# Seven block products for eight in the gated linear unit and the down projection, with the first pair of each FFN made plain

## The chip, the cores and the metric

The kernel runs on one core of one Trainium2 chip. Its metric is the device time of one execution in microseconds (us). The engines are named as the profile names them: PE multiplies matrices (PEld is its weight load), DVE and ACT work on vectors, POOL is GpSimd, and SP issues most of the loads.

## The reference

Two blocks run one after the other on `x` of 256 rows and 2048 columns, in fp32. The first has a state-space mixer whose output goes through a gated linear unit (GLU), an attention over dilated windows, and after each of them a feed-forward network (FFN). The second has two layers of a mixer of its own kind, which the change doesn't touch. What it touches, cut down:

```python
def swiglu_ffn(h, w_gate_up, w_down):            # d = 2048, d_ff = 5632
    gate, up = jnp.split(h @ w_gate_up, 2, axis=-1)
    return (jax.nn.silu(gate) * up) @ w_down

def s5_mixer(u, a_re, a_im, log_dt, b_re, b_im, c_re, c_im, d_skip, w_glu):
    ...
    g = jax.nn.gelu(y).astype(u.dtype)           # y: the outputs of the scan
    val, gate = jnp.split(g @ w_glu, 2, axis=-1)
    return (val.astype(f32) * jax.nn.sigmoid(gate.astype(f32))).astype(u.dtype)

def first_block(x, ...):
    for layer in range(2):
        h = rmsnorm(x, mix_norm[layer])
        x = x + (s5_mixer(h, ...) if layer == 0 else dilated_attention(h, ...))
        x = x + swiglu_ffn(rmsnorm(x, ffn_norm[layer]), w_gate_up[layer], w_down[layer])
    return x
```

## The kernel before, in words

**Stages.** The program is one stream: the state-space mixer (`s5`, lines 405 to 890), the GLU (893 to 911), the FFN of layer 0 (328 to 356), the attention, the FFN of layer 1, and the two mixers of the second block. `x` stays in the core's memory as 2 row halves of 128 rows. For a product, 128x128 blocks of it are transposed on PE, and gain and split make the left operand: a k-tile is 128 of the 2048 columns.

**Products.** Every fp32 operand is split in two parts, hi (a cast on ACT) and lo (a subtraction on DVE), so that a product takes three matmuls: hi times hi, hi times lo of the weights, lo times hi. `gemm` (55 to 90) makes one block of 512 columns: 16 k-tiles, 2 row halves, 3 matmuls, 96 in all (lines 69, 70, 71), into 2 of the 4 banks of the pool `psg`. Its weights come in `load_unit` (30 to 47) as 4 k-tiles a load of 1 MB, by SP into 2 buffers `wraw`, and are split 2 k-tiles at a time (42, 43) into 4 buffers each of `whi` and `wlo`.

**Seven for eight.** `Strassen.gemm_pair` (144 to 221) makes two blocks of 512 columns together. Of 4 k-tiles, 12 to 15, it takes 2x2 blocks (row halves, and even and odd k-tiles, on the left; even and odd k-tiles, and the two column blocks, on the right) and forms seven products of sums of blocks where eight plain ones would stand, each 6 matmuls (168 to 170). The sums of weights are DVE subtractions into `wt` (3 buffers), split like weights (140, 141). Four intermediate results are copied out of their bank by ACT (line 174) into `st_p1`, `st_p7`, `st_u2` and `st_u4`, one buffer each, because the bank goes on to sum. The other 12 k-tiles are plain (212 to 214, 144 matmuls): 186 matmuls for a pair, where two calls of `gemm` have 192. At the end DVE adds the four copies to the four banks.

**The FFN.** Before its first product `x_transposed` (306 to 324) transposes k-tiles 12 to 15 first (line 315), makes of them the left operands of the seven products (`x_pair`, 112 to 133, with the copies and sums on ACT and DVE), and then transposes k-tiles 0 to 11 (line 259). There are 11 chunks of 512 columns of d_ff, in groups of 4, 4 and 3. Each chunk is a `gemm_pair` of a gate block and an up block; its product, `m`, is transposed during the next pair (8 transposes, `meanwhile`). After a group the down projection runs four plain calls of `gemm` over the 16 (last group 12) k-tiles of the group, and each adds its two banks to `x` (line 355). The GLU runs 8 plain calls.

**Order.** A scheduler that works by priority lays out each engine's instructions, and each engine runs its own in order. `meanwhile` and `start` queue work, of which a call of a product takes pieces as it goes; `behind` puts an instruction after another one. The weight loads of a next product are issued when a buffer is free.

**State-space mixer.** It starts with loads on two queues: four of `x` on SP (447, 448), six small ones (`dt`, `ai`, `ar`) on ACT's queue, and then on ACT's queue the gains and `b_re`, `b_im`. At its end DVE runs a serial scan, while PE makes kernel matrices, which go through memory (`kp`) into `M` (795, 798); then PE makes the outputs from `M` (`own`) and from the scan's states (`states`), and ACT and DVE split them for the GLU. `load_x` (800) loads `x` anew behind that.

## Time and profile before

| | |
|---|---|
| median of 3 runs | 3247.86 us (3246.82 to 3248.42) |
| the profiled execution, its own time | 3248.64 us |
| its span in the profile | 3246.5 us |
| granted TensorE clock, mean | 0.994 |
| busy: PE, DVE, ACT | 97%, 65%, 51% of the span |
| HBM read | 568.51 MB, 176 GB/s |

The span is the time from the first to the last instruction, 2.1 us less than the execution. Busy shares count overlapping work of several engines, each by itself. A pipelined matmul's listed duration reaches beyond the start of the next one, so the pace of matmuls is taken from the distance of starts. In a timeline row, brackets give how long the engine had been idle and what released it. The clock column is 1.00 where PE was granted its full 2.4 GHz throughout.

### The profile page before, as it was taken

What the parts mean: (1) busy time and instruction counts of PE and PEld (TensorE: products, weight loads), DVE (VectorE), ACT (ScalarE), POOL (GpSimd) and SP (SyncE); (2) the same over time, 40 slices, a digit from 0 to 9 for tenths busy, and PEclk for the clock granted to TensorE, in tenths of its full rate; (3) what the DMA queues carried; (4) which work ended last, traced back from release to release, by engine and by line L of the source; (5) the groups of instructions that cost most, each with busy time, mean ns of one, the idle gap of its engine ahead of it and who ended that gap; (6) DMA issues with size and microseconds to landing.
All of it is one profiled execution on the core that took longest, in us unless ns stands there. A gap on an engine that the chain in (4) does not pass through costs nothing.

```text
span 3246.5 us, 43041 instructions
## 1 busy us (share of the span) xinstructions
PE 3162.5 (97%) x16950; PEld 2689.0 (83%) x16961; DVE 2121.9 (65%) x3244; ACT 1668.9 (51%) x2247; POOL 13.7 (0%) x23
## 2 busy tenths in 40 slices
PE   4999999999999999999989999999999999999998
PEld 4788788888888888888878888888889888899887
DVE  8955776576575666756778757756657566575565
ACT  6344654455454555545555545545456455564463
POOL 1000000000000000000000000000000000000000
PEclk9999999999999999999999999999999999999999
DMA  3265456555555555454555646555555546556554
GB/s 72 59 214 191 141 207 208 195 194 195 190 176 199 169 171 176 159 189 162 169 163 195 205 169 207 205 188 203 172 175 166 190 151 214 162 165 194 161 185 168
DMA packets 341675, 573.93 MB, mean 177 GB/s; under 512 B 53537, under 2 KB 105249, under 8 KB 340641
## 3 DMA queue, kind: packets, MB, share of 16 engines
q1 hardware_dynamic: 306944, 561.84, 52.7%
q10 hardware_dynamic: 34528, 9.35, 1.4%
q8 instruction: 133, 2.18, 0.3%
q14 instruction: 70, 0.57, 0.1%
HBM read 568.51 MB, written 2.62 MB: 176 GB/s over the span
## 4 chain that ended last, share of the span: by engine, by line
PE 92%; ACT 3%; DVE 2%; DMA 2%; issue 1%; ACTq 0%; another core or an unknown queue 0%; DVEq 0%; SPq 0%
PE psg L71 19%; PE psg L69 19%; PE psg L70 19%; PE psg L214 7%; PE psg L213 7%; PE psg L212 7%; PE psg L168 2%; PE psg L169 2%; PE psg L170 2%; PE psm L378 2%; PE psg L378 1%; PE psm L259 1%; PE psm L1012 1%; DMA wraw<-in_w_in 1%; ACT act_hi L268 1%
## 5 line engine op out<-in xcount | busy, mean ns | idle before, releaser
L43 DVE TENSOR_TENSOR wlo<-wraw,whi 128x1024 fp32r<-128x1024 f32 (+1 forms) x752 | 863.5, 1155 | 727.6 <-ACT whi L42 723.2
L42 ACT CAST whi<-wraw 128x1024 fp32r<-128x1024 f32 (+1 forms) x752 | 744.3, 997 | 941.4 <-PE psg L71 664.0
L69 PE MATMUL psg<-whi,act_hi 128*128 128x512 f32 (+1 forms) x2912 | 1101.4, 378 | 0.8 <-DVE act_lo L378 0.7
L71 PE MATMUL psg<-whi,act_lo 128*128 128x512 f32 (+1 forms) x2912 | 1094.4, 376 | 0.2
L70 PE MATMUL psg<-wlo,act_hi 128*128 128x512 f32 (+1 forms) x2912 | 1093.8, 376 | 0.0
L71 PEld LDWEIGHTS psg<-whi,act_lo 128*128 128x128 f32 x2912 | 546.8, 188 | 85.9 <-issue 1.3
L69 PEld LDWEIGHTS psg<-whi,act_hi 128*128 128x128 f32 x2912 | 547.2, 188 | 85.4 <-issue 1.3
L70 PEld LDWEIGHTS psg<-wlo,act_hi 128*128 128x128 f32 x2912 | 547.3, 188 | 81.9
L141 DVE TENSOR_TENSOR wlo<-wraw,whi 128x1024 fp32r<-128x1024 f32 x330 | 393.6, 1222 | 225.8 <-ACT whi L140 224.9
L140 ACT CAST whi<-wraw 128x1024 fp32r<-128x1024 f32 x330 | 339.6, 1054 | 328.5 <-DMA wraw<-in_w_gate_up 171.3
L212 PE MATMUL psg<-whi,act_hi 128*128 128x512 f32 x1056 | 412.2, 390 | 0.0
L214 PE MATMUL psg<-whi,act_lo 128*128 128x512 f32 x1056 | 411.1, 389 | 0.0
L213 PE MATMUL psg<-wlo,act_hi 128*128 128x512 f32 x1056 | 410.9, 389 | 0.0
L214 PEld LDWEIGHTS psg<-whi,act_lo 128*128 128x128 f32 x1056 | 198.2, 188 | 41.2
L212 PEld LDWEIGHTS psg<-whi,act_hi 128*128 128x128 f32 x1056 | 198.3, 188 | 40.8
L213 PEld LDWEIGHTS psg<-wlo,act_hi 128*128 128x128 f32 x1056 | 198.3, 188 | 40.8
L141 DVE TENSOR_TENSOR wlo<-wt,whi 128x1024 fp32r<-128x1024 f32 x88 | 107.3, 1220 | 33.3 <-ACT whi L140 33.3
L168 PE MATMUL psg<-whi,xf_hi 128*128 128x512 f32 x308 | 122.1, 405 | 6.8 <-ACT st_p L174 5.8
L140 ACT CAST whi<-wt 128x1024 fp32r<-128x1024 f32 x88 | 92.8, 1054 | 66.0 <-PE psg L214 36.5
L169 PE MATMUL psg<-wlo,xf_hi 128*128 128x512 f32 x308 | 123.5, 401 | 0.0
L170 PE MATMUL psg<-whi,xf_lo 128*128 128x512 f32 x308 | 122.4, 398 | 0.2 <-DVE xf_lo L131 0.2
L168 PEld LDWEIGHTS psg<-whi,xf_hi 128*128 128x128 f32 x308 | 59.2, 192 | 23.0 <-ACT st_p L174 6.6
(350 smaller groups left out, 2374.4 us busy)
## 6 DMA issues: line engine op xcount, KB each, us to landing
wraw<-in_w_gate_up SPq DMA_DIRECT2D x352, 512.0 KB, 4.7
wraw<-in_w_down SPq DMA_DIRECT2D x88, 1024.0 KB, 5.0
wraw<-in_w_in SPq DMA_DIRECT2D x96, 768.0 KB, 4.6
wraw<-in_w_q SPq DMA_DIRECT2D x48, 1024.0 KB, 5.2
wraw<-in_w_glu SPq DMA_DIRECT2D x32, 1024.0 KB, 5.4
wraw<-in_w_kv SPq DMA_DIRECT2D x32, 1024.0 KB, 5.4
wraw<-in_w_in SPq DMA_DIRECT2D x32, 1024.0 KB, 5.1
wraw<-in_w_out SPq DMA_DIRECT2D x32, 1024.0 KB, 5.1
```

The costliest lines, as they stand in the source:

```text
L42: k.act_at = nc.scalar.copy(hi[:, :n, :cw], raw[:, a:a + n, :cw]).ins
L43: k.dve_at = nc.vector.tensor_tensor(lo[:, :n, :cw], raw[:, a:a + n, :cw], hi[:, :n, :cw].bitcast(F32), ALU.subtract).ins
L69: nc.tensor.matmul(o, a, wh, start=n == 0, stop=False)
L70: nc.tensor.matmul(o, a, wl, start=False, stop=False)
L71: k.mm = nc.tensor.matmul(o, b, wh, start=False, stop=n == total - 1).ins
L140: k.act_at = nc.scalar.copy(hi, src).ins
L141: k.dve_at = nc.vector.tensor_tensor(lo, src, hi.bitcast(F32), ALU.subtract).ins
L168: nc.tensor.matmul(o, a, wh[:, q], start=start and q == 0, stop=False, skip_group_check=True)
L169: nc.tensor.matmul(o, a, wl[:, q], start=False, stop=False, skip_group_check=True)
L212: nc.tensor.matmul(o, a, wh[:, n], start=False, stop=False, skip_group_check=True)
L213: nc.tensor.matmul(o, a, wl[:, n], start=False, stop=False, skip_group_check=True)
L214: k.mm = nc.tensor.matmul(o, b, wh[:, n], start=False, stop=end, skip_group_check=True).ins
```

## The change

It does five things.

1. The GLU's last three column blocks go through `gemm_pair` (gate and value block as the pair); the first stays plain.
2. The down projection goes through `gemm_pair` twice a group, on column blocks 0 and 1, then 2 and 3. Its block k-tiles are the first four of the group, whose sums (`mf`) are made as soon as the group's first chunk is transposed. With `apart`, the four kept copies aren't added to the banks: copies and banks are each added to `x`, 8 DVE additions a pair in place of 4.
3. The first pair of each FFN is plain (`gemm` for gate, `gemm` for up). The sums for the later ones are made beside it by the new `forms`, from the finished hi and lo. Single blocks (A11, A12, A22) are taken from the operand itself.
4. `load_x` goes behind the first GLU product, and the first GLU weights are issued behind the last load of `M` (`k.sp_at`).
5. The six small loads at the start go from ACT's queue to SP's, ahead of `x`.

The pieces of queued work in `gemm_pair` are now taken once after the seven products and after every fourth direct k-tile.

```diff
 in gemm:
-        with behind(k, k.lo_at):
+        with behind(k, k.lo_at), behind(k, k.sp_at):
             parts = load_unit(k, W, g[0][1], len(g), c0, cw)
 in Strassen (x_forms and x_pair are removed):
+    def forms(self, xT, kt0, name):
+        k, nc = self.k, self.k.nc
+        xh, xl = (x[:, kt0:kt0 + 4, :] for x in xT)
+        hi, lo = (self.pool.tile([128, 4, 2, 128], F32R, name=f"{name}_{n}") for n in ("hi", "lo"))
+        x = self.block().rearrange("p q (i t) -> p (q i) t", i=2)
+        nc.vector.tensor_tensor(x, xh.bitcast(F32), xl.bitcast(F32), ALU.add)
+        x = x.rearrange("p (q i) t -> p q i t", i=2)
+        a11, a12, a21, a22 = (x[:, :, i, t * 128:(t + 1) * 128] for t in range(2) for i in range(2))
+        sm = self.block().rearrange("p a (b t) -> p (a b) t", t=128).rearrange("p (f q) t -> p f q t", q=2)
         nc.vector.tensor_tensor(sm[:, 0], a21, a22, ALU.add)
         nc.vector.tensor_tensor(sm[:, 2], a11, a21, ALU.subtract)
         nc.vector.tensor_tensor(sm[:, 1], sm[:, 0], a11, ALU.subtract)
         nc.vector.tensor_tensor(sm[:, 3], a12, sm[:, 1], ALU.subtract)
+        nc.scalar.copy(hi, sm)
+        nc.vector.tensor_tensor(lo, sm, hi.bitcast(F32), ALU.subtract)
+        return kt0, hi, lo
 in gemm_pair, after the direct k-tiles:
+        if apart:
+            return banks, ((p1, u4), (u2, p7))
         for o, e in ((c22, p7), (c21, u2), (c11, p1), (c12, u4)):
             nc.vector.tensor_tensor(o, o, e, ALU.add)
 in ffn:
-    xT, forms = x_transposed(k, gain, 1, st)
+    xT = x_transposed(k, gain, 1)
...
-            ps = st.gemm_pair(xT, forms, wgu, 0, (c * 512, dff + c * 512))
+            if c == 0:
+                pg = gemm(k, xT, kgroups(), wgu, 0, 512)
+                sils = [silu(t, pg[t]) for t in range(2)]
+                forms = st.forms(xT, 12, "xf")
+                pu = gemm(k, xT, kgroups(), wgu, dff, 512)
...
+            else:
+                ps = st.gemm_pair(xT, forms, range(KT), wgu, 0, (c * 512, dff + c * 512))
...
+                if c == s0:
+                    mforms.append(st.forms(mid, 0, "mf"))
...
-        for nn in range(4):
-            pd = gemm(k, mid, kgroups(4 * n, s0 * 512), wd, nn * 512, 512)
+        for nn in range(0, 4, 2):
+            pd, rest = st.gemm_pair(
+                mid, mforms[-1], range(4 * n), wd, s0 * 512, (nn * 512, nn * 512 + 512), apart=True
+            )
+            for of in (rest, pd):
+                for t in (1, 0):
+                    for j in range(2):
+                        xs = k.x[:, t, (nn + j) * 512:(nn + j + 1) * 512]
+                        nc.vector.tensor_tensor(xs, xs, of[t][j], ALU.add)
 in s5:
-            k.nc.scalar.dma_start(dt[r], I["ssm_log_dt"][0].rearrange("(a g) -> g a", a=2))
+            nc.sync.dma_start(dt[r], I["ssm_log_dt"][0].rearrange("(a g) -> g a", a=2))
...
-                nc.sync.dma_start(M[r0:r0 + 16, half * 32:half * 32 + 32, 16 * j:], kp[:, :, 0:w])
+                k.sp_at = nc.sync.dma_start(M[r0:r0 + 16, half * 32:half * 32 + 32, 16 * j:], kp[:, :, 0:w]).ins
-
-    load_x(k)
 in glu:
-    for n in range(4):
-        pg = gemm(k, gT, groups, w, D + n * 512, 512)
...
+    pg = gemm(k, gT, groups, w, D, 512)
+    with behind(k, k.sp_at):
+        load_x(k)
+    k.lo_at = k.sp_at = None
+    sig = [sigmoid(t, pg[t]) for t in range(2)]
+    forms = st.forms(gT, 12, "xf")
+    pv = gemm(k, gT, groups, w, 0, 512)
...
+    for n in range(1, 4):
+        ps = st.gemm_pair(gT, forms, range(KT), w, 0, (D + n * 512, n * 512))
```

The change moves instructions in places that a diff line doesn't show. On PE, at the start of the FFN of layer 1, the rows before are these (`xf` are the sums of the left operand, `act` its split k-tiles, `x` and `ident` make a transpose):

```order
L71 MATMUL psg<-whi,act_lo 128x512
L315 MATMUL psm<-ident,x 128x128 x2
L259 MATMUL psm<-ident,x 128x128 x4
L315 MATMUL psm<-ident,x 128x128 x6
L259 MATMUL psm<-ident,x 128x128 x8
L168 MATMUL psg<-whi,xf_hi 128x512
L169 MATMUL psg<-wlo,xf_hi 128x512
L170 MATMUL psg<-whi,xf_lo 128x512
L168 MATMUL psg<-whi,xf_hi 128x512
```

Now, in the same place (line 269 is the transpose, 69 to 71 are `gemm`):

```order
L71 MATMUL psg<-whi,act_lo 128x512
L269 MATMUL psm<-ident,x 128x128 x16
L69 MATMUL psg<-whi,act_hi 128x512
L70 MATMUL psg<-wlo,act_hi 128x512
L69 MATMUL psg<-whi,act_hi 128x512
L70 MATMUL psg<-wlo,act_hi 128x512
L71 MATMUL psg<-whi,act_lo 128x512 x2
L69 MATMUL psg<-whi,act_hi 128x512
L70 MATMUL psg<-wlo,act_hi 128x512
L69 MATMUL psg<-whi,act_hi 128x512
L269 MATMUL psm<-ident,x 128x128 x12
```

The first product's matmuls now stand among the transposes of plain k-tiles, with no product of sums ahead of them.

On SP, at the end of the state-space mixer, before (`kd` to `kp` to `M` is the way of the kernel matrices; rows in between are left out):

```order
L475 DMA s5d_88<-in_ssm_d 128x16
L1521 DMA x_71<-in_x 128x2048 x2
L33 DMA wraw_2723<-in_w_glu 128x4x512
L33 DMA wraw_2757<-in_w_glu 128x4x512
L795 DMA kp00_1185<-kd_1180 16x512 x4
L795 DMA kp01_1266<-kd_1261 16x512 x3
L798 DMA M_1109<-kp00_1185 16x2048
```

Now, around the last load of `M`:

```order
L819 DMA M_1109<-kp11_1428 16x32x32
L819 DMA M_1109<-kp11_1428 16x32x16
L33 DMA wraw_2724<-in_w_glu 128x4x512
L33 DMA wraw_2758<-in_w_glu 128x4x512
L1553 DMA x_71<-in_x 128x2048 x2
L33 DMA wraw_2792<-in_w_glu 128x4x512
```

`x` and the first two GLU loads stood ahead of all stores and loads of `kp` and `M` and now stand behind them.

On DVE, where one down projection pair ends and the next begins, now (`wt` are sums of weights, line 376 adds to `x`; rows further on repeat):

```order
L155 TENSOR_TENSOR wt<-wraw_5702,wt 128x1024
L133 TENSOR_TENSOR wlo<-wraw,whi 128x1024 x4
L133 TENSOR_TENSOR wlo<-wraw_5702,whi 128x1024
L133 TENSOR_TENSOR wlo<-wt,whi 128x1024
L376 TENSOR_TENSOR x<-x,psg 128x512 x2
L155 TENSOR_TENSOR wt<-wraw_5702,wt 128x1024
L376 TENSOR_TENSOR x<-x,psg 128x512
L133 TENSOR_TENSOR wlo<-wt,whi 128x1024
L376 TENSOR_TENSOR x<-x,psg 128x512
L133 TENSOR_TENSOR wlo<-wt,whi 128x1024
L133 TENSOR_TENSOR wlo<-wraw_5702,whi 128x1024
L376 TENSOR_TENSOR x<-x,st_p_5735 128x512
```

The additions that empty the banks of the pair before stand among the splits of the next pair's sums, and the kept copies of the next pair are added in the middle of its direct k-tiles.

## Rows read from the trace of the kernel before

**Rows 1.** The page: busy time of each engine, then the chain's shares by engine.
```profile
PE 3162.5 (97%) x16950; PEld 2689.0 (83%) x16961; DVE 2121.9 (65%) x3244; ACT 1668.9 (51%) x2247; POOL 13.7 (0%) x23
...
PE 92%; ACT 3%; DVE 2%; DMA 2%; issue 1%; ACTq 0%; another core or an unknown queue 0%; DVEq 0%; SPq 0%
```

**Rows 2.** Windows: stretch, length, busy PE PEld DVE ACT POOL, clock, DMA share, GB/s.
```profile
417.34:460.51 43.17, 43.17 (x197) 35.76 (x195) 31.74 (x31) 23.34 (x28) 0.00 (x0) 1.00 0.57 196
588.00:631.50 43.50, 43.50 (x193) 35.94 (x192) 25.97 (x24) 21.23 (x24) 0.00 (x0) 1.00 0.51 171
1744.18:1788.35 44.17, 43.72 (x197) 35.59 (x195) 36.91 (x78) 27.16 (x33) 0.00 (x0) 1.00 0.56 190
```

**Rows 3.** Chain of waits, FFN of layer 0: the same transposes, start and us.
```profile
417.34 0.87 PE psm L259 x8
...
460.51 0.87 PE psm L259 x8
...
677.01 0.87 PE psm L259 x8
```

**Rows 4.** PE's timeline around such transposes: the matmuls just before and behind them.
```profile
416.95 0.40 PE L214 MATMUL psg<-whi,act_lo 128*128 128x512 f32 x1
...
417.97 0.48 PE L212 MATMUL psg<-whi,act_hi 128*128 128x512 f32 x1
```

**Rows 5.** PE's timeline at both FFN starts: last GLU or attention product to first direct.
```profile
340.99 0.39 PE L71 MATMUL psg<-whi,act_lo 128*128 128x512 f32 x1
...
354.39 0.80 PE L168 MATMUL psg<-whi,xf_hi 128*128 128x512 f32 x1 [2.90 <-ACT st_p L174]
...
363.99 0.40 PE L212 MATMUL psg<-whi,act_hi 128*128 128x512 f32 x1
...
1663.37 0.39 PE L71 MATMUL psg<-whi,act_lo 128*128 128x512 f32 x1
...
1668.44 0.69 PE L315 MATMUL psm<-ident,x 128*128 128x128 f32 x2 [4.68 <-DVE x L1073]
...
1690.65 0.39 PE L212 MATMUL psg<-whi,act_hi 128*128 128x512 f32 x1
```

**Rows 6.** Windows: a stretch of the FFN start of layer 0.
```profile
350.00:360.00 10.00, 7.09 (x21) 5.11 (x21) 5.26 (x12) 9.03 (x20) 0.00 (x0) 0.66 0.00 0
```

**Rows 7.** PE's timeline at the start of the first mixer, which is plain.
```profile
2397.65 0.39 PE L71 MATMUL psg<-whi,act_lo 128*128 128x512 f32 x1
...
2405.58 0.34 PE L69 MATMUL psg<-whi,act_hi 128*128 128x384 f32 x1
...
2415.99 0.33 PE L69 MATMUL psg<-whi,act_hi 128*128 128x384 f32 x1
```

**Rows 8.** DVE's timeline at the start of the program.
```profile
16.10 1.23 DVE L378 TENSOR_TENSOR x<-x,s5gain 128x1024 f32<-128x1024 f32 x1 [3.67 <-DMA x<-in_ssm_b_re]
...
18.20 1.23 DVE L378 TENSOR_TENSOR x<-x,s5gain 128x1024 f32<-128x1024 f32 x1 [0.67 <-DMA x<-in_ssm_b_im]
```

**Rows 9.** Timeline at the end of the state-space mixer, SP's queue (SPq), PE and DVE.
```profile
105.63 0.94 SPq L33 DMA_DIRECT2D wraw<-in_w_glu  x2
...
113.68 0.42 PE L378 MATMUL psm<-VW,bT 64*16 64x64 f32 x13 [3.25 <-issue]
...
117.36 2.96 SPq L798 DMA_DIRECT2D M<-kp  x4
...
150.44 0.48 DVE L378 TENSOR_TENSOR S<-S,sc 128x64 f32<-128x64 f32 x2
...
154.75 4.06 PE L378 MATMUL psm<-VW,S 64*64 64x64 f32 x128
```

**Rows 10.** Lines by form: the down projection's additions; busy, mean ns, idle before.
```profile
L355 DVE TENSOR_TENSOR x<-x,psg 128x512 f32<-128x512 f32 x48 | 30.9, 681 | 1.1 <-PE psg L71 1.1
```

**Rows 11.** The page's DMA issues: count, KB each, median us to landing.
```profile
wraw<-in_w_gate_up SPq DMA_DIRECT2D x352, 512.0 KB, 4.7
wraw<-in_w_down SPq DMA_DIRECT2D x88, 1024.0 KB, 5.0
```

More of the change, by code (lines that the diff above doesn't have):

```diff
@@ L175, in kept @@
             return e
-        product(c22, "A11", *self.split(b11), True)
+        product(c22, "A11", b11, True)
         p1 = kept(c22, "st_p1")
-        product(c21, "S3", *self.split(total(b22, b12)), True)
+        product(c21, "S3", total(b22, b12), True)
         p7 = kept(c21, "st_p7")
@@ L182, in gemm_pair, with jobs @@
         t2 = total(b22, t1)
-        product(c22, "S2", *self.split(t2), False)
+        product(c22, "S2", t2, False)
         u2 = kept(c22, "st_u2")
-        product(c21, "-A22", *self.split(total(t2, b21)), False)
-        product(c11, "A12", *self.split(b21), True)
-        product(c22, "S1", *self.split(t1), False)
+        product(c21, "A22", total(b21, t2), False)
+        product(c11, "A12", b21, True)
+        product(c22, "S1", t1, False)
         u4 = kept(c22, "st_u4")
-        product(c12, "S4", *self.split(b22), True)
-        dh, dl = xT
+        product(c12, "S4", b22, True)
+        direct = [kt for kt in kts if not kt0 <= kt < kt0 + 4]
+        calls = 1 + len(direct) // 4
+        called = 0
+        def jobs():
+            nonlocal called
+            called += 1
+            for job, rate in list(k.jobs):
+                for _ in range(8 * rate * called // calls - 8 * rate * (called - 1) // calls):
+                    next(job, None)
+        jobs()
         banks = ((c11, c12), (c21, c22))
-        last = self.DIRECT // 2 - 1
-        for i in range(last + 1):
+        last = len(direct) // 2 - 1
+        for g in range(last + 1):
             raw = k.wraw.tile([128, 4, 512], F32, name="wraw").rearrange("p (i n) c -> p i n c", n=2)
-            r0 = row0 + i * 256
+            pair = direct[2 * g:2 * g + 2]
+            r0 = row0 + pair[0] * 128
             for n, c0 in enumerate(cols):
@@ L202, in gemm_pair @@
             order = [(j, t) for j in range(2) for t in range(2)]
-            if i == last:
+            if g == last:
                 order = [(j, t) for t in (1, 0) for j in range(2)]
@@ L206, in gemm_pair @@
                 wh, wl = parts[j]
-                kt = 2 * i + j
-                a, b = dh[:, kt, t * 128:(t + 1) * 128], dl[:, kt, t * 128:(t + 1) * 128]
+                a, b = (x[:, pair[j], t * 128:(t + 1) * 128] for x in xT)
                 for n in range(2):
-                    end = i == last and j == 1
                     o = banks[t][n]
@@ L213, in gemm_pair @@
                     nc.tensor.matmul(o, a, wl[:, n], start=False, stop=False, skip_group_check=True)
-                    k.mm = nc.tensor.matmul(o, b, wh[:, n], start=False, stop=end, skip_group_check=True).ins
-            if i % 2:
-                for job, rate in list(k.jobs):
-                    for _ in range(rate * 8 // 6 if i < last else rate * 8 - 2 * (rate * 8 // 6)):
-                        next(job, None)
+                    k.mm = nc.tensor.matmul(
+                        o, b, wh[:, n], start=False, stop=g == last and j == 1, skip_group_check=True
+                    ).ins
+            if g % 2:
+                jobs()
+        if apart:
+            return banks, ((p1, u4), (u2, p7))
         for o, e in ((c22, p7), (c21, u2), (c11, p1), (c12, u4)):
@@ L351, in ffn, with gated @@
-        for nn in range(4):
-            pd = gemm(k, mid, kgroups(4 * n, s0 * 512), wd, nn * 512, 512)
-            for t in range(2):
-                xs = k.x[:, t, nn * 512:(nn + 1) * 512]
-                nc.vector.tensor_tensor(xs, xs, pd[t], ALU.add)
+                nc.scalar.activation(sil, g, AF.Silu, scale=rstd[:, t:t + 1])
+                return sil
+            def gated(t, u, sil):
+                nc.vector.scalar_tensor_tensor(m[:, t, :], u, rstd[:, t:t + 1], sil, ALU.mult, ALU.mult)
@@ L456, in s5 @@
             )
+    for j in range(4):
+        nc.sync.dma_start(xs[:, j, :], xr[:, j, :])
     for half in range(2):
```

115 lines of the change are left out of this document (45 added, 70 removed).

## The prediction

> **What bounds the kernel now.** I read the page's busy times and chain first: PE is busy for 97% of the span and carries 92% of the chain that ended last, while DVE stands at 65% and ACT at 51% [rows 1]. So a matmul taken away is worth its pitch wherever DVE, ACT and the loads keep up, and only the few stretches where PE waits can give more. Next the windows [rows 2]: an FFN pair with seven products lasts 43.17 us, with PE busy in all of it, DVE in 31.74, ACT in 23.34. A pair of plain down projection blocks lasts 43.50, DVE 25.97. The chain shows that this goes on unbroken: the same 8 transposes come every 43.17 us, and the next group begins 259.67 us later [rows 3], which is four pairs (172.7) and 87.0 for the down projection, 43.5 for two blocks. Then I looked for where PE waits, in its timeline at both FFN starts [rows 5] and the state-space mixer's timeline [rows 8, 9].
>
> **Prices.** A plain pair has 192 matmuls: 43.50 / 192 = 0.2266 us each [rows 2]. The 8 transposes of a gate and up pair cost 417.97 − 416.95 − 0.23 = 0.79 us, 0.099 each [rows 4]. Without them the pair with seven products lasts 43.17 − 0.79 = 42.38.
>
> **1. Seven for eight in more pairs: −14.5.** Added are 12 such pairs in the down projections (3 groups, 2 layers, 2 pairs) and 3 in the GLU; lost are the first pairs of the two FFNs; net 13. Each saves 43.50 − 42.38 = 1.12 us, measured from pairs that exist and that include their waits for copies and sums. 13 × 1.12 = 14.6, taken as 14.5. The best end is 6 matmuls × 0.2266 = 1.36 (−17.7). The other end takes off half of the 1.00 us by which the gate and up pair with the fullest DVE is longer than a usual one (44.17 against 43.17, DVE 36.91 [rows 2]): 0.62 each, −8.
>
> What covers it? DVE must have room for it: the added sums and splits make a down pair like a gate and up pair, so about 32 us of 42. It also gets eight additions to `x`, which it had before (0.681 us each [rows 10]). The four kept copies go to `x` directly, so no addition stands between the last product and the emptying of a bank except the eight themselves; on DVE they stand between splits of the next pair. The next pair's first bank needs only the first of them.
>
> **2. The FFN starts: −21.3.** From the end of the last matmul of the stage before (start + 0.23) to the first direct k-tile is 363.99 − 341.22 = 22.77 us in layer 0 and 1690.65 − 1663.60 = 27.05 in layer 1 [rows 5]. At full pace the stretch holds 42 matmuls (9.52) and 32 transposes (3.17), 12.7 us; 10.0 and 14.3 are lost. The rows name it: in layer 1 PE waits 4.68 us for the last columns of `x`, since k-tiles 12 to 15 are wanted first; then a product waits 2.90 us for ACT's copy of a result, ACT being busy 9.03 of 10 us with copies, gains and splits; and the granted clock of that stretch is 0.66, so part of it runs at 1.2 GHz [rows 6].
>
> The change puts plain products there, on k-tiles in their natural order, and needs no sums. The nearest row for that is the start of the first mixer, which is plain and mixes transposes and products the same way: 2405.58 − 2397.88 = 7.70 us for 21 matmuls of 384 columns (0.1735 each, from 60 of them between 2405.58 and 2415.99) and 32 transposes, together 6.81 [rows 7]. It loses 0.9. I take 2.0 lost in layer 0, whose last transposes wait for the additions behind a GLU pair, and 1.0 in layer 1: 8.0 + 13.3 = 21.3. Ends: all 24.3, or half of it, 12. The new sums are made by `forms` beside the up block: two DVE operations of 1024 columns (1.23 each [rows 8]) and four of 256, at most 0.68 each [rows 10]. That is 4 to 5 us of DVE in 43 us that leave it 17; nothing waits for it but a product 20 us later.
>
> **3. The mixer's start: −2.4.** DVE waits 3.67 us for `b_re` and 0.67 for `b_im` [rows 8]. The six small issues ahead of them on ACT's queue go to SP's, so `b` starts earlier; on SP they stand ahead of `x`, and what reads `x` comes later for that. The wait that can go is 4.34; a delay of `x` can give half of it back or, if `x` decides, all of it and 2 more. I take a little over half of 4.34; ends +2 and −4.3.
>
> **4. The mixer's end: −3.7.** SP issues GLU weights at 105.63 and the first load of `M` only at 117.36; PE idles 3.25 us before 113.68; the scan ends at 150.92, but the first product that reads it starts at 154.75, 3.83 us later [rows 9]. With `x` and 2 MB of GLU weights behind `M`, PE's work on `M` comes earlier and the scan sets the time. I take 3.7 of the 3.83. The other end is +3, about PE's idle time there again, if the first GLU weights, now issued after the last `M`, arrive late.
>
> **5. What comes back: +4.0.** The sums `mf` add 4 to 5 us of DVE to the second pair of each group. In layer 1 one such pair already holds table work (DVE 36.91 of 44.17 [rows 2]); 41 of 42.4 leaves no slack, and I give it 2.5. The pairs of a last group have 12 k-tiles, so 48 fewer direct matmuls (10.9 us) to hide the same sums: +1. The attention now starts behind a GLU pair whose last columns come together: +0.5.
>
> Sum: −14.5 − 21.3 − 2.4 − 3.7 + 4.0 = −37.9. The profiled execution took 3248.64, so 3210.7; the median of the runs stands 0.8 below the profiled one, at 3247.86, so **3210**.
>
> **A rule on loads.** The down projection's loads go from 1024 KB an issue to 512 KB, 16 a pair. The 512 KB loads of the gate and up weights land in 4.7 us, the 1024 KB ones in 5.0 [rows 11], and the pairs with the smaller ones move 196 GB/s with PE never idle [rows 2]. The Trainium skill's page "DMA: Bandwidth & Descriptors" (section "Measured (HBM→SBUF, 128 partitions, SWDGE, issued from GpSimd)") says to batch loads to 1 MiB or more for three quarters of the peak, and its section "Anatomy of one DMA" gives 2 us fixed plus size over 436 GB/s for a load. By that a 512 KB load is an estimated 3.2 us, 16 of them one after the other 51, more than the pair lasts, and 15 pairs would lose some 130 us. The trace disagrees: in the pairs that exist such loads overlap without a wait of PE.
>
> **The rivals.**
>
> *Starts give only half.* ACT still makes all gains and splits of `x`, and was the busy engine there (9.03 of 10 [rows 6]). Then 12 us more: 3222. For it: the 16 k-tiles have as many splits as before, and two plain blocks want weights split too. Against: the mixer's start does the same work and loses 0.9 [rows 7].
>
> *The mixer gains nothing*, since `b` and `x` or `M` and the GLU weights only change places: 6.1 us more, 3216.
>
> *Slower: kept copies block the next pair.* There is one buffer for each kept copy. Before, the final additions freed them; with `apart`, additions to `x` do, on a fuller DVE in order. If these come late, ACT's copy of the next pair waits, and with it the bank and PE. Price of such a wait: 2.90 us [rows 5], and the clock falls behind it: at 0.66 over 10 us [rows 6] some 6.8 us ran at half, which loses 3.4, of which I count half, 1.7. 12 pairs × 4.6 = 55: 3266. It is slower than before, by more than 0.2%, from (37.9 + 6.5) / 12 = 3.7 us a pair on. Against it: in the order of the change the additions of the copies stand in the middle of the same pair's direct k-tiles, some 20 us ahead of the next copy.
>
> *Loads one at a time* (the rule above, as a mechanism). Loads of 512 KB would queue up: 16 × 4.7 = 75.2 us a pair [rows 11], 32.8 more than 42.4, in 15 pairs: some 490 more, about 3700. The 22 existing pairs exclude this nearly.
>
> *The change doesn't do what it says:* pairs on the DVE limit save nothing and starts only move their wait behind the first pair: −3 to −8, 3240 to 3245.
>
> **Chances.** My forecast 60%; starts half 14%; mixer nothing 14%; more gained than summed (under 3202: bank waits of 1.36 a pair, starts without loss) 4%; no real effect 3%; slower by copies 4%; loads 1%. The range, 3202 to 3226, takes in the forecast, the two partial cases and the low end of the pairs (+6.5), and leaves out some 12 to 18%. About 0.2%, 6.5 us, is what a measurement tells from no change: faster by more 0.93, within it 0.03, slower by more 0.04.
>
> **What would show it.** Right: a chain period of down pairs near 42.4 us where it was 43.5 (in a last group near 42.4 − 10.9 = 31.5); 10 and 14 us of loss at FFN starts shrunk to some 2 and 1, no copy wait there, a clock near 1.00; DVE's `b` waits shorter than 4.34 in sum; states within 0.5 us of the scan's end. Wrong: down pairs over 43.5 with PE idle in front of a product behind ACT's copy or DVE's sum; a new PE wait at 12 us or more in a start; a load as the releaser of PE in the down projection.

## The result

Changed kernel 3208.86 us (median of 4 runs, 3207.84 to 3210.05), before 3247.34: ratio 0.9881, 95% interval 0.9864 to 0.9898. In a second set of runs of the same two kernels the ratio was 0.9870 (0.9855 to 0.9885). The forecast was 3210 with a range of 3202 to 3226.

The profiled execution took 3209.36 us, its span 3207.6 (before 3246.5), its mean clock 0.996. Parts 1 and 4 of the changed kernel's page, as [rows 1]:

```profile
PE 3137.0 (98%) x16872; PEld 2671.6 (83%) x16883; DVE 2277.0 (71%) x3421; ACT 1728.8 (54%) x2335; POOL 13.8 (0%) x23
...
PE 91%; DVE 3%; ACT 3%; DMA 2%; issue 0%; SPq 0%; ACTq 0%; another core or an unknown queue 0%; DVEq 0%
```

PE is busy for 25.5 us less in a span that is 38.9 us shorter; the rest was waiting. DVE took on 155 us.

Where it went shows best by stage. The lengths run from the start of a stage's last matmul to that of the next stage's, as PE's timeline has them (the first: to the first GLU product). The last column is a second profile of the changed kernel.

| stage | before | changed | difference | changed, again |
|---|---|---|---|---|
| state-space mixer | 166.00 | 161.14 | −4.86 | 161.30 |
| GLU | 174.99 | 173.65 | −1.34 | 173.66 |
| FFN, layer 0 | 727.27 | 708.74 | −18.53 | 708.68 |
| attention | 595.11 | 594.56 | −0.55 | 594.71 |
| FFN, layer 1 | 734.28 | 716.98 | −17.30 | 716.10 |
| first mixer | 417.60 | 420.48 | +2.88 | 416.83 |
| second mixer | 422.21 | 423.04 | +0.83 | 422.57 |

**The pairs.** Windows of the changed kernel, as [rows 2], in layer 0: the second down projection pair of a group, the gate and up pair behind it (which has no transposes), and a usual gate and up pair with 8 transposes. Then two of layer 1: the pair that has both table work and the sums `mf`, and a second down pair.

```profile
552.58:594.80 42.22, 42.22 (x188) 34.91 (x187) 31.91 (x32) 21.31 (x23) 0.00 (x0) 1.00 0.59 200
594.80:637.01 42.21, 42.21 (x188) 34.91 (x186) 29.80 (x29) 22.11 (x24) 0.00 (x0) 1.00 0.58 199
432.99:476.10 43.11, 43.11 (x196) 35.74 (x195) 31.93 (x32) 23.47 (x28) 0.00 (x0) 1.00 0.58 196
1687.63:1730.87 43.24, 43.24 (x195) 35.75 (x194) 41.28 (x87) 27.35 (x33) 0.00 (x0) 1.00 0.56 195
1860.61:1902.94 42.33, 42.33 (x187) 34.92 (x186) 31.86 (x32) 21.30 (x23) 0.00 (x0) 1.00 0.61 199
```

A down pair without transposes is 42.22 us where two plain blocks took 43.50, with PE busy throughout and DVE at 32, as forecast. That is 1.3 us a pair in layer 0. In layer 1, where the same pairs are 0.1 us longer, it is 1.2. The loads of half the size don't show:

```profile
wraw<-in_w_down SPq DMA_DIRECT2D x176, 512.0 KB, 5.1
```

(page, DMA issues) they land in 5.1 us, where 1024 KB took 5.0 [rows 11], and no wait of PE in a full pair names one.

**The FFN starts.** PE's timeline of the changed kernel from the last GLU product to the first product of sums, then the same after the attention, as [rows 5]:

```profile
334.79 0.39 PE L222 MATMUL psg<-whi,act_lo 128*128 128x512 f32 x1
335.02 0.82 PE L269 MATMUL psm<-ident,x 128*128 128x128 f32 x6
...
380.12 0.39 PE L166 MATMUL psg<-whi,act_hi 128*128 128x512 f32 x1
...
1638.09 0.39 PE L71 MATMUL psg<-whi,act_lo 128*128 128x512 f32 x1
1638.32 1.91 PE L269 MATMUL psm<-ident,x 128*128 128x128 f32 x16
...
1643.05 0.73 PE L71 MATMUL psg<-whi,act_lo 128*128 128x512 f32 x2 [1.46 <-DVE act_lo L279]
...
1687.63 0.39 PE L166 MATMUL psg<-whi,act_hi 128*128 128x512 f32 x1
```

In layer 0 the plain pair takes 380.12 − 335.02 = 45.10 us. It holds 192 matmuls (43.5) and the last 14 transposes (1.4): 0.2 lost. The other 18 transposes ran inside two GLU pairs, which last 43.51 us for it where the first lasts 42.21: 2.6 for 18, and at 0.1 each 0.8 of that is loss too. In layer 1 it is 49.31 against 46.7 (192 matmuls, 32 transposes): 2.6 lost, 1.46 of it in one wait for DVE. Before, 10.0 and 14.3 were lost. Layer 0's figure repeats in every run with that start behind GLU pairs. Layer 1's is one execution's: in the twelve profiles with a plain first pair it is 1.8 to 5.3. In both starts of the changed kernel the granted clock stays at full. In layer 0 DVE and ACT are nearly always busy and the loads run at 345 GB/s (window of the changed kernel, as [rows 6]):

```profile
335.02:345.02 10.00, 10.00 (x53) 8.46 (x52) 9.93 (x17) 9.10 (x22) 0.00 (x0) 1.00 0.97 345
```

**The seam to the first mixer** is where time came back, in a place that the prediction didn't name. Timeline of the changed kernel there (`subln` is the gain of a norm inside the mixer, `lruv` a small parameter of it):

```profile
2336.30 5.73 ACTq L1349 DMA_DIRECT2D lruv<-in_lru_conv_b  x1
2342.14 1.04 ACT L132 CAST whi<-wraw 128x1024 fp32r<-128x1024 f32 x1 [9.30 <-issue]
...
2344.50 0.50 PE L221 MATMUL psg<-wlo,act_hi 128*128 128x512 f32 x1 [0.76 <-DVE wlo L133]
...
2357.47 0.23 DVE L1490 TENSOR_SCALAR subln<-subln 128x128 f32<-128x128 f32 x1 [1.75 <-DMA subln<-in_diff_subln_g]
...
2360.21 0.69 PE L71 MATMUL psg<-whi,act_lo 128*128 128x384 f32 x1 [2.65 <-DVE act_lo L279]
```

Small loads of the mixer stand on ACT's queue among the casts of the last down pair's weights. One issue holds ACT for 5.73 us, and PE waits behind the late casts. Then a DVE instruction on another small load stands between the additions to `x`; DVE waits 1.75 us for it and PE 2.65, and the granted clock of 2344 to 2364 is 0.91. Before, the same DVE instruction did not wait.

### The profile page after: what moved, and what is told of

Read it like the earlier page. It is cut to its first block, busy times and chain, and to the rows that moved or that the text cites. A ratio compares the mean times of both kernels' runs of the same rounds, so it can differ in the third digit from the quotient of the medians.

```text
span 3207.6 us, 43406 instructions
## 1 busy us (share of the span) xinstructions
PE 3137.0 (98%) x16872; PEld 2671.6 (83%) x16883; DVE 2277.0 (71%) x3421; ACT 1728.8 (54%) x2335; POOL 13.8 (0%) x23
## 4 chain that ended last, share of the span: by engine, by line
PE 91%; DVE 3%; ACT 3%; DMA 2%; issue 0%; SPq 0%; ACTq 0%; another core or an unknown queue 0%; DVEq 0%
PE psg L71 14%; PE psg L69 14%; PE psg L70 14%; PE psg L220 11%; PE psg L221 11%; PE psg L222 11%; PE psg L166 4%; PE psg L167 3%; PE psg L168 3%; PE psm L269 1%; PE psg L399 1%; DMA wraw<-in_w_in 1%; DVE S L399 1%; PE psm L1044 1%; DVE sc L399 1%; ACT VW L399 1%
## 5 line engine op out<-in xcount | busy, mean ns | idle before, releaser
L43 DVE TENSOR_TENSOR wlo<-wraw,whi 128x1024 fp32r<-128x1024 f32 (+1 forms) x560 | 628.1, 1131 | 467.9 <-ACT whi L42 466.6
L42 ACT CAST whi<-wraw 128x1024 fp32r<-128x1024 f32 (+1 forms) x560 | 540.8, 978 | 640.1 <-PE psg L71 377.1
L133 DVE TENSOR_TENSOR wlo<-wraw,whi 128x1024 fp32r<-128x1024 f32 x509 | 608.4, 1222 | 279.5 <-ACT whi L132 277.1
L69 PE MATMUL psg<-whi,act_hi 128*128 128x512 f32 (+1 forms) x2144 | 802.8, 374 | 0.9 <-DVE act_lo L399 0.7
L71 PE MATMUL psg<-whi,act_lo 128*128 128x512 f32 (+1 forms) x2144 | 796.4, 372 | 4.1 <-DVE act_lo L279 4.1
L70 PE MATMUL psg<-wlo,act_hi 128*128 128x512 f32 (+1 forms) x2144 | 796.2, 371 | 0.8 <-DVE wlo L43 0.8
L132 ACT CAST whi<-wraw 128x1024 fp32r<-128x1024 f32 x509 | 522.8, 1055 | 488.7 <-DMA wraw<-in_w_gate_up 168.5
L220 PE MATMUL psg<-whi,act_hi 128*128 128x512 f32 x1616 | 630.8, 390 | 0.8 <-ACT whi L132 0.8
L221 PE MATMUL psg<-wlo,act_hi 128*128 128x512 f32 x1616 | 628.9, 389 | 0.8 <-DVE wlo L133 0.8
L222 PE MATMUL psg<-whi,act_lo 128*128 128x512 f32 x1616 | 628.8, 389 | 0.0
L168 PE MATMUL psg<-whi,act_lo 128*128 128x512 f32 x210 | 82.0, 390 | 0.0
L167 PE MATMUL psg<-wlo,act_hi 128*128 128x512 f32 x210 | 81.9, 390 | 0.0
```

Of the source, the lines that this page charges most:

```text
L42: k.act_at = nc.scalar.copy(hi[:, :n, :cw], raw[:, a:a + n, :cw]).ins
L43: k.dve_at = nc.vector.tensor_tensor(lo[:, :n, :cw], raw[:, a:a + n, :cw], hi[:, :n, :cw].bitcast(F32), ALU.subtract).ins
L69: nc.tensor.matmul(o, a, wh, start=n == 0, stop=False)
L70: nc.tensor.matmul(o, a, wl, start=False, stop=False)
L71: k.mm = nc.tensor.matmul(o, b, wh, start=False, stop=n == total - 1).ins
L132: k.act_at = nc.scalar.copy(hi, src).ins
```

## The experiments

My theory was that of the prediction: pairs at PE's pace, starts freed of sums, two smaller gains in the state-space mixer. The rivals stood in each expectation. All intervals below are 95%, and ratios are against the kernel before.

**1. Down projection plain.**

```diff
-        for nn in range(0, 4, 2):
-            pd, rest = st.gemm_pair(mid, mforms[-1], ..., apart=True)
+        for nn in range(4):
+            pd = gemm(k, mid, kgroups(4 * n, s0 * 512), wd, nn * 512, 512)
```

> The changed kernel (3208.9 us) with only the down projection plain again: no sums of the group's first chunk, four plain calls a group. Theory: each of the 12 pairs loses 43.50 - 42.21 = 1.29 us and pays for nothing else, so the down projections take 12 x 1.29 = 15.5 us longer. The first mixer's start, 4.3 us longer in the changed kernel because DVE waits there for a small load, should be as before, which gives 4.3 back: 3208.9 + 15.5 - 4.3 = 3220. Rival (the fuller DVE and the smaller loads of the new pairs cost the stages around them something): the FFN stages outside the down projection get shorter too, and the total is 3212 to 3216.

3219.44 us, ratio 0.9911 (0.9896 to 0.9926). FFN of layer 0: 716.52, 7.78 longer, 1.30 for each of 6 pairs. Layer 1: 722.95, 5.97 longer: 7.1 for six pairs and 1.0 at its start (3.7 lost there in this run), less the 2.0 that the last pair lost at the seam. First mixer 416.12. The rival, that the rest of the FFN gets shorter, is not borne out: the gate and up pairs keep their 43.11 and 43.23 us.

**2. GLU plain.**

```diff
-        ps = st.gemm_pair(gT, forms, range(KT), w, 0, (D + n * 512, n * 512))
+        pg = gemm(k, gT, groups, w, D + n * 512, 512)
+        pv = gemm(k, gT, groups, w, n * 512, 512)
```

> The changed kernel with only the gated linear unit plain again. Theory: 3 x 1.29 = 3.9 us longer, 3212.8, the first FFN's start unchanged within 1 us because its transposes of finished columns go on among the plain products. Rival (the good start of the first FFN rests on the pairs, which finish their columns in another order and leave room for transposes): 2 us or more on top, 3215 or more, with a PE wait at the FFN's start.

3212.71, ratio 0.9891 (0.9876 to 0.9905). GLU and FFN of layer 0 together 887.07 us against 882.39, 4.7 longer. The GLU's three blocks and the first FFN pair are 4.0 longer together, close to the 3.9 of the forecast. Most of the rest, 0.65, is in the last down pair of the layer, which waits 0.31 for ACT's copy. The GLU by itself is only 1.34 longer, because its transposes go back to the FFN, whose start is 47.8 us with all 32 (1.1 lost). So the pairs are not what makes the start good.

**3. First FFN pair with seven products, k-tiles 12 to 15 first.**

```diff
-            if c == 0:
-                pg = gemm(k, xT, kgroups(), wgu, 0, 512)
...
+    for kts in ([12, 13, 14, 15], list(range(12))):
+        split_transposed(k, lambda t, i, kts=kts: ..., xT, kts, gain)
+        if kts[0] == 12:
+            forms = st.forms(xT, 12, "xf")
```

> The changed kernel with seven products in the first FFN pair again: k-tiles 12 to 15 are transposed first, the sums are made by the new form of the code from them, then come k-tiles 0 to 11. Theory (the start is paid for by sums and late columns ahead of the first product): the two FFN starts take back most of their 21 us less the 2 x 1.29 that two more pairs gain: 3224 to 3230, with waits of 2 us or more on DVE's or ACT's sums and a low clock. Rival (what was slow before was the old way of making the sums, gain and copies on ACT, not their place): 3208 to 3214.

3238.37, ratio 0.9970 (0.9959 to 0.9981), above the theory's 3230. The FFNs are 728.51 and 727.65, 19.8 and 10.7 longer. PE's timeline and the windows at both starts:

```profile
341.81 2.75 PE L269 MATMUL psm<-ident,x 128*128 128x128 f32 x16 [2.32 <-DVE x L925]
...
354.95 0.79 PE L167 MATMUL psg<-wlo,act_hi 128*128 128x512 f32 x1 [4.11 <-DVE wlo L133]
...
1677.19 0.80 PE L166 MATMUL psg<-whi,xf_hi 128*128 128x512 f32 x1 [5.29 <-ACT whi L132]
```

```profile
342.00:364.00 22.00, 14.17 (x49) 9.53 (x49) 19.56 (x33) 17.54 (x37) 0.00 (x0) 0.60 0.30 91
1666.00:1684.00 18.00, 8.44 (x32) 5.43 (x32) 17.06 (x28) 13.93 (x27) 0.00 (x0) 0.72 0.06 1
```

The columns of `x` that come last are wanted first, then DVE and ACT have splits, gains, sums and weights in one row, PE waits, and the granted clock is 0.60 and 0.72 over these two stretches. The new way of making sums is no help there; its place beside plain products is.

**4. First pair plain, without the rest of the change.** The kernel has the old GLU, down projection and state-space mixer; the new inside of `gemm_pair` stays.

```diff
-            ps = st.gemm_pair(xT, forms, ...)
+            if c == 0:
+                pg = gemm(k, xT, kgroups(), wgu, 0, 512)
+                forms = st.forms(xT, 12, "xf")
+                pu = gemm(k, xT, kgroups(), wgu, dff, 512)
```

> The kernel before with one part of the change alone: the first pair of each FFN is plain and the sums are made beside it; GLU, down projection and state-space mixer are as before. Theory (the starts are worth 21.5 us, and two pairs give back 1.29 each): 19 us less than before, ratio 0.994; the first seven-product pair begins 45 to 47 us behind the last GLU product in layer 0 and 47 to 49.5 behind the attention in layer 1. Rival (the starts are quick only because the GLU pairs let transposes go ahead): layer 0 gains 5 us or less, ratio 0.996 or more.

3229.47, ratio 0.9941 (0.9928 to 0.9955), 19.3 us less than before. The FFNs are 8.06 and 10.35 shorter, together 18.4. Layer 0's start, with plain GLU blocks:

```profile
341.41 0.39 PE L71 MATMUL psg<-whi,act_lo 128*128 128x512 f32 x1
341.64 1.91 PE L269 MATMUL psm<-ident,x 128*128 128x128 f32 x16
...
389.46 0.39 PE L166 MATMUL psg<-whi,act_hi 128*128 128x512 f32 x1
```

47.82 us with all 32 transposes in it, 1.1 lost. Layer 1's pair takes 51.3 us from its first transposes, 2 more than in the changed kernel: the same wait of 1.47 us for DVE is there, and this time the granted clock was lower, 0.88 from 1657.0 to 1671.7. So the two starts give back 8.9 and 9.7, less the 2.5 that two lost pairs cost. The last 2 us of the FFNs' gain come from the other gate and up pairs, which the new inside makes a little shorter, as in the changed kernel. So half of the whole gain, 19.3 of 38.5 us, is in this run, and the GLU pairs matter little for it.

**5. Kept copies added to the banks, then the banks to x.** Eight additions a pair, as in the changed kernel, in another order.

```diff
-            for of in (rest, pd):
-                ... nc.vector.tensor_tensor(xs, xs, of[t][j], ALU.add)
+            pd = st.gemm_pair(mid, mforms[-1], ...)
+            ... nc.vector.tensor_tensor(xs, xs, pd[t][j], ALU.add)
```

> The changed kernel with the kept copies of the down projection added into the banks first, and the banks then to x, as gate and up pairs do it; 8 additions a pair as before. Theory (DVE has room, and the banks of the second row half come free first): a down pair stays within 0.3 us of 42.2; the total is 3205 to 3212, the lower end because the small load in front of the first mixer then stands elsewhere on DVE. Rival (keeping them apart is what lets the next pair start at once): 1 us or more a pair, 3221 and more, with a wait for DVE in front of a pair's first products.

3232.22, ratio 0.9943 (0.9928 to 0.9957). My theory fell and the rival held: the FFNs are 722.23 and 730.29, 13.5 and 13.3 longer. In the first two groups of a layer, the second down pair and the gate and up pair behind it last 44.8 to 44.9 us, where the changed kernel has 42.2 to 42.3: 2.6 for each of eight pairs, twice what a pair gains. The rest is 2.9 in the last down pair of layer 0, which here has 16 transposes of the next stage in it, and 2.7 at the start of layer 1's FFN, which scatters as much. Timeline at the end of a group's second down pair, where a gate and up pair begins, first this run, then the changed kernel (the border between the two down pairs, at 549.4, has the same row of eight):

```profile
594.26 0.69 DVE L230 TENSOR_TENSOR psg<-psg,st_u 128x512 f32<-128x512 f32 x1
594.86 0.69 DVE L230 TENSOR_TENSOR psg<-psg,st_p 128x512 f32<-128x512 f32 x1
595.46 1.27 DVE L373 TENSOR_TENSOR x<-x,psg 128x512 f32<-128x512 f32 x2
596.80 0.70 DVE L230 TENSOR_TENSOR psg<-psg,st_p 128x512 f32<-128x512 f32 x1
597.48 0.70 DVE L230 TENSOR_TENSOR psg<-psg,st_u 128x512 f32<-128x512 f32 x1
598.09 1.27 DVE L373 TENSOR_TENSOR x<-x,psg 128x512 f32<-128x512 f32 x2
599.28 1.22 DVE L133 TENSOR_TENSOR wlo<-wt,whi 128x1024 fp32r<-128x1024 f32 x1
600.42 1.22 DVE L155 TENSOR_TENSOR wt<-wraw,wt 128x1024 f32<-128x1024 f32 x1
...
602.82 0.50 PE L166 MATMUL psg<-whi,act_hi 128*128 128x512 f32 x1 [0.84 <-ACT whi L132]
...
604.08 0.51 PE L167 MATMUL psg<-wlo,act_hi 128*128 128x512 f32 x1 [0.76 <-DVE wlo L133]
```

```profile
591.78 1.28 DVE L376 TENSOR_TENSOR x<-x,psg 128x512 f32<-128x512 f32 x2
592.98 1.22 DVE L155 TENSOR_TENSOR wt<-wraw,wt 128x1024 f32<-128x1024 f32 x1
594.32 0.69 DVE L376 TENSOR_TENSOR x<-x,psg 128x512 f32<-128x512 f32 x1
594.92 1.22 DVE L133 TENSOR_TENSOR wlo<-wt,whi 128x1024 fp32r<-128x1024 f32 x1
```

Eight additions in one row hold DVE for 5 us; the sum of weights for the next product (`wt`) starts at 600.42, behind all of them, where the changed kernel slips it between the additions. ACT's cast and DVE's split come after it, and PE waits twice, 0.84 and 0.76. From first to last start the seven products take 11.97 us instead of 9.35. DVE is no busier than in the changed kernel (2276.3 us against 2277.0): it is the order at the border that costs.

**6. Start of the state-space mixer: the six small loads back on ACT's queue.**

```diff
+    for j in range(4):
+        nc.sync.dma_start(xs[:, j, :], xr[:, j, :])
-        nc.sync.dma_start(dt[r], ...)
+        k.nc.scalar.dma_start(dt[r], ...)
```

> The changed kernel with the six small loads at the start back on ACT's queue, ahead of b, and x first on SP's. Theory (b sets the start): DVE waits 3 us or more for b_re and b_im again, PE's first transposes begin at 38 to 41 us instead of 36 to 38, the scan ends as much later, and the total is 2 to 3.5 us longer, 3211 to 3212.5. Rival (the start is set by when the loads land, which varies by more from run to run, not by their order): no shift of the median beyond 1 us.

**7. Its end: x and the first GLU weights ahead of kp and M.**

```diff
+    load_x(k)
+    k.sp_at = None
```

> The changed kernel with x loaded anew and the first two GLU weights issued ahead of the stores and loads of kp and M again. Theory: the first load of M is issued 7 to 11 us later, PE idles 3 us in the kernel matrices, and the GLU's first product comes 15 us behind the scan's end instead of 13.4: 1.5 us longer, 3210.4. Rival (the prediction's term of 3.7): 3212.5. Other rival (the scan alone decides): 3209.

**8. Both together.**

> The changed kernel with both load orders of the state-space mixer put back (the six small loads on ACT's queue, x and the first GLU weights ahead of kp and M). Theory: the first GLU product at 165 to 167 us in the profile as in the kernel before, where nine profiles of kernels with the new orders lie at 159 to 166 with a mean near 162; 3 to 4 us longer in the medians, a ratio near 0.9885 against 0.987 to 0.988. Rival (only scatter): 161 to 163 and a ratio below 0.988.

3209.46 (ratio 0.9878), 3208.89 (0.9873) and 3211.90 (0.9887, 0.9874 to 0.9901). The medians can't tell them from the changed kernel's 0.9870 and 0.9881; only the profiles help. With both old orders (before, and experiments 4 and 8) the first GLU product comes at 166.0, 166.4 and 167.3. With both new ones nine profiles have 158.8 to 165.9, mean 162.2. So 4.4 us, with a scatter of 7 from profile to profile. Experiment 6 has 165.35 in its one profile and experiment 7 has 166.4: with one old order each, neither shows the early product.

The stage can be cut where DVE's scan ends, because from PE's first transposes to there all fourteen profiles have 111.2 to 111.3 us. The first transposes are at 39.7 to 39.9 in the four profiles with the old start and at 35.6 to 40.3, mean 37.1, in the ten with the new one: 2.7 are the start's. From the scan's end to the first GLU product it is 15.1 to 16.3, mean 15.7, in the four with the old end and 11.4 to 15.9, mean 14.1, in the ten with the new one: 1.6 are the end's. The scatter of the start has a cause that shows: the last piece of `b_im` lands at 12.3 to 13.0 us in six of the ten, and DVE doesn't wait for it; in the other four it lands at 15.2 to 18.0, and DVE waits 0.6 to 3.3. PE's first row, the changed kernel's first and then that of experiment 8:

```profile
36.48 3.75 PE L399 MATMUL psg<-ident,VW 64*128 64x64 f32 x33 [36.48 <-ACT VW L399]
```

```profile
39.83 0.45 PE L399 MATMUL psg<-ident,VW 64*128 64x64 f32 x2 [39.83 <-ACT VW L399]
```

**9 to 12. The seam to the first mixer.** First the constant on the sub-norm gain folded into its use, so that DVE's early instruction is gone:

```diff
-        nc.vector.tensor_scalar(sg, sg, 1.0 - lam_init(l), None, ALU.mult)
...
-            nc.vector.tensor_tensor(mv[:, t], mv[:, t], sg..., ALU.mult)
+            nc.vector.scalar_tensor_tensor(mv[:, t], mv[:, t], 1.0 - lam_init(l), sg..., ALU.mult, ALU.mult)
```

> The changed kernel with one DVE instruction less in each mixer: the constant on the sub-norm gain is folded into the product that uses it, so DVE no longer waits for that small load between the last additions to x. Theory: the 1.75 us wait of DVE, the 2.65 us wait of PE behind it and the stretch at half clock go, 3 to 4.3 us: 3204.6 to 3206. Rival (the start is slow because the last 1024 columns of x come together and DVE has four additions there): less than 1 us, 3208 to 3209.

3207.01, ratio 0.9874 (0.9859 to 0.9889); first mixer 416.64. That looked like the theory, but the last pair's direct part (its plain k-tiles, behind the seven products) is 25.4 us here, where the changed kernel has 23.7. And then the changed kernel was profiled again:

> The changed kernel as it is, for the scatter of its stages from profile to profile. Theory: the FFN and attention stages repeat within 0.3 us, while the state-space mixer (161.1 us to the first GLU product) and the last down pair with the first mixer's start scatter by 3 us or more, since both hang on when small loads land. Rival: everything repeats within 0.5 us, so that stage differences of 2 us between the earlier runs are effects of their edits.

3206.58, ratio 0.9870; first mixer 416.83, with the DVE instruction in the same place and a smaller wait:

```profile
2354.71 0.23 DVE L1490 TENSOR_SCALAR subln<-subln 128x128 f32<-128x128 f32 x1 [1.07 <-DMA subln<-in_diff_subln_g]
2357.45 0.44 PE L71 MATMUL psg<-whi,act_lo 128*128 128x384 f32 x1 [0.50 <-DVE act_lo L279]
```

So the wait comes with the change and its size with the execution: DVE waits 0.3 to 1.8 us there in all seven profiles that have the changed kernel's loads and DVE instruction at this seam, and PE 0.3 to 2.7 behind it. Folding the constant takes it away, but the medians don't show a gain. ACT's block is there in both, too:

```profile
2336.79 4.58 ACTq L1349 DMA_DIRECT2D lruv<-in_lru_conv_b  x1
2341.49 1.05 ACT L132 CAST whi<-wraw 128x1024 fp32r<-128x1024 f32 x1 [8.49 <-issue]
```

(timeline of the second profile) with the last pair's direct part at 23.0 us, 23.7 in the first profile, where 21.65 is usual in a last group. Next the mixers' small loads put behind the first mixer product's casts:

```diff
     project("lx", lx)
+    k.par_at = k.act_at
...
+        with behind(k, k.par_at):
             nc.scalar.dma_start(cw_, ...)
```

> The changed kernel with the small loads of the mixers (convolution, gates, decay, sub-norm gain), which ACT issued among the weight casts of the last down projection pair, put behind the first mixer product's casts. Theory: ACT no longer stands 9 us on an issue and DVE no longer waits for the sub-norm gain, so the last pair takes 31.4 us instead of 33.5 and the first mixer loses 3 to 4 us less: 3203 to 3204. Rival (these loads then come late for the mixers): the mixers take 3 us or more longer, 3208 or more. Other rival (only the wait of DVE counted, and ACT's casts had slack): 3206, as in the run that only folded the constant.

3211.23, ratio 0.9877 (0.9860 to 0.9893). The last pair's direct part is 21.5 us, as the theory had it, and the FFN 714.79, the shortest of all. But the first mixer takes 421.80, 5 more than in the second profile: the second half of the forecast failed, and the rival's number came. Its reason is shown in part only: PE has one new wait, of 2.1 us, for a cast on ACT.

```profile
PE psm L1381 <- ACT whi L42: 2.1, 1, 2.1
```

Last, the same loads issued by POOL, with the constant folded:

```diff
-            nc.scalar.dma_start(vec[:, i, :], ...)
+            nc.gpsimd.dma_start(vec[:, i, :], ...)
```

> The changed kernel with the constant folded as in the earlier run, and the small loads of the mixers issued by POOL, which is idle, in place of ACT: they stay early, but no cast of weights stands behind them on ACT's queue. Theory (both kinds of wait at the seam of the FFN and the first mixer are queueing behind small loads): the last down pair 31.4 us (9.46 + 21.6 + 0.3) and the first mixer 416 to 417 us, where the changed kernel's profile has 33.4 and 420.5: about 5 us less in the profile than the changed kernel profiled beside it, 3 to 6 in the medians. Rival (the loads of POOL are slower to issue or DVE suffers from them): first mixer 419 or more, no gain beyond 1 us.

3205.14, ratio 0.9865 (0.9848 to 0.9881), no different from the changed kernel's 3206.58 beside it. Last direct part 21.5 again, but the first mixer 422.00, with 4.3 us of waits for its first operands. POOL's issues of these small loads took 0.5 to 1.6 us each, so they were not slow. But the mixer's first weights took 12.0 us to land, where the changed kernel's two profiles have 4.7 and 6.1, and ACT cast them late, ahead of these operands. Why they took so long is not shown:

```profile
PE psg L69 <- ACT act_hi L278: 4.3, 2, 2.4
```

So in both runs the mixer took back what the last pair gained. I found no version that is faster than the changed kernel beyond the intervals.

## Why the prediction was right

The total was right, 3210 against 3208.86 and 3206.58. Its two large terms are shown by experiments; the small ones were partly wrong and cancelled.

1. **Pairs, −14.5: some −16.3.** Worked out from 1.30 for each of 6 down pairs in layer 0, 1.19 in layer 1, 1.29 for 3 in the GLU, less 1.25 for each of 2 lost. The mechanism held (experiments 1 and 2), the size was short by 0.07 to 0.18 a pair. The term that was mis-sized is the price of 8 transposes. I took the start of the matmul behind them as their end [rows 4], but the next matmul of the kernel before starts 0.32 us later and not 0.23:

```profile
417.97 0.48 PE L212 MATMUL psg<-whi,act_hi 128*128 128x512 f32 x1
418.29 0.39 PE L213 MATMUL psg<-wlo,act_hi 128*128 128x512 f32 x1
```

   The changed kernel shows the whole price, a pair with and without them: 43.11 − 42.21 = 0.90, not 0.79. The kernel before has such a pair too, the first of a group:

```profile
526.15:614.09 87.94, 87.94 (x393) 72.91 (x392) 47.94 (x46) 35.30 (x35) 0.00 (x0) 1.00 0.55 186
614.09:656.34 42.25, 42.25 (x187) 34.91 (x186) 28.92 (x28) 21.88 (x24) 0.00 (x0) 1.00 0.60 199
```

   (windows of the kernel before, as [rows 2]: a down projection, then the gate and up pair behind it.) The window 588.00:631.50, which the prediction reads as a pair of down projection blocks, reaches 17 us into this gate and up pair, so its DVE figure is a mixture. Its 43.50 is right all the same: four blocks and 8 transposes are 87.94, and (87.94 − 0.90) / 2 = 43.52. In the chain of [rows 3] the two slips cancel: one of the four pairs has no transposes, and the down projection has them. The lower end, 0.62 a pair for a full DVE, was not reached: the fullest pair, with DVE at 41.3, takes 43.24, as the others of its layer do. It was read from a pair that did not show it. Its window, 1744.18:1788.35, spans halves of two pairs, and the one with the fuller DVE is not the long one, which waited 0.45 for a cast (windows of the kernel before):

```profile
1723.32:1766.69 43.37, 43.37 (x195) 35.75 (x194) 39.55 (x82) 27.05 (x33) 0.00 (x0) 1.00 0.57 194
1766.69:1810.85 44.16, 43.71 (x196) 35.59 (x195) 34.10 (x47) 23.65 (x27) 0.00 (x0) 1.00 0.56 191
```

2. **FFN starts, −21.3: 9.0 + 11.7 = −20.7 measured** in the first profile, in other shares (8.0 and 13.3) and with the loss inside the GLU pairs counted. The start of experiment 4 gives 8.9 + 9.7 = 18.6. So the size is good to the 3.5 us by which layer 1's start scatters. Experiment 3 shows the cause by putting it back. The nearest row, the mixer's plain start [rows 7], was a good guide in layer 0: it lost 0.9, this loses 1.0. Layer 1's lost 2.6.

3. **Mixer's start, −2.4: −2.7** as a mean over profiles, with a scatter as large. The mechanism held: in the changed kernel's profile DVE's two waits for `b` are gone, and where `b_im` lands late one of them is back.

4. **Mixer's end, −3.7: some −1.6.** The step that failed is that with `x` and the GLU weights behind `M` the scan sets the time, and the 3.83 us between its end and the product that reads it [rows 9] go. PE spends them on work that is left over, and most of it stays. In the changed kernel the scan ends at 147.73 and the same product starts at 150.17, still 2.44 behind:

```profile
148.33 1.91 PE L399 MATMUL psg<-ident,kd 128*128 128x128 f32 x16
150.17 4.06 PE L399 MATMUL psm<-VW,S 64*64 64x64 f32 x128
```

   PE runs other outputs and transposes up to it, nearly without idle time. The granted clock, which the prediction didn't look at here, differs too: from 105 us to this product it is 0.83 to 0.86 in the four profiles with the old end and 0.89 to 1.00 in the ten with the new one. How much of the 1.6 is the clock's is not shown. Once, in experiment 9's profile, the product stands 0.45 behind the scan's end, as the prediction had it; in the others with the new end 2.4 to 5.0.

5. **What comes back, +4.0: right in size by luck, wrong in place.** The sums `mf` cost no wait (43.24 in the pair with the tables, where its neighbours in layer 1 take 43.23), the last groups none (31.4 us for the pair without transposes, where 31.5 was forecast), and the attention came out 0.55 shorter. What came back is at the seam behind the last down pair: 1.4 to 2.0 us in that pair in both profiles, and 3.7 more in the two mixers in the first profile alone. The prediction followed the moved loads on SP's queue and didn't look at ACT's at the FFN's end, where the mixers' small loads stand among the casts; before, the same issue took 1.93 us and PE did not wait. Against it stand some 2 us that the prediction didn't have: the other gate and up pairs became shorter (43.16 to 43.11 in layer 0, 43.34 to 43.23 in layer 1, and one that had waited 0.45 for a cast from 44.15 to 43.27).

The rivals: the starts did not stay by half. (That rival was priced 3 us too high: with half of 24.3 instead of 21.3 it is 9 us more, 3219, not 12.) Loads of 512 KB did not queue up: 16 of them pass in a down pair of 42.2 us at 200 GB/s, and PE waits for none. So the Trainium skill's rule in "DMA: Bandwidth & Descriptors", section "Measured (HBM→SBUF, 128 partitions, SWDGE, issued from GpSimd)", to batch loads to 1 MiB or more, has no price here. The slower rival had the wrong object but the right place: no kept copy blocked a down pair of the changed kernel, yet experiment 5 shows that DVE's additions at the end of a down pair can take back 2.6 us a pair, twice its gain, if they stand in one row.

## What to carry to other kernels

When an algorithm saves matmuls by sums, the first use of it at a stage's start may cost more than it saves: make the first product plain and the sums beside it. Where PE is the bound, look at what one engine does in a row at the border of two products; the same eight additions cost nothing or 2.6 us a pair by their order and grouping. Before a gain or loss of a few us is put down to an edit, profile the same kernel twice, and cut a stage where one part of it repeats.

## What was not expected of the hardware

The issue of one small load held ACT for 5.73 and 4.58 us in the two profiles of the changed kernel, and for 4.7 to 5.5 in the six other runs that have it at the same place; where it stands earlier, it took 1.9. Why is open. The start of the program scatters by over 4 us between profiles of the same instructions there (35.6 to 40.3 us to PE's first transposes), with the landing of one load (12.3 to 18.0 us), while the FFN of layer 0 repeats within 0.6 us over the eight profiles with the same code in it. And the granted clock at the start of layer 0's FFN was 0.60 in experiment 3, where PE was busy for 14.17 of 22.00 us, and 1.00 in the changed kernel, where it was busy throughout.
